# A residual tile generator queued two gate blocks later, and a smaller credit for the retention generators

## The chip, the cores and the metric

The kernel runs on one core of a Trainium2 chip. The metric is the time of one execution on the device in microseconds (us). Several executions of each kernel are timed and the median is taken; one further execution is recorded by the hardware profiler.

TensorE (PE) multiplies matrices; its weight loads (PEld) overlap its matmuls. VectorE (DVE), ScalarE (ACT) and GpSimd (POOL) do the elementwise work, and SyncE (SP) issues most of the DMA transfers. Each engine takes its instructions strictly in the order of the program that was written for it.

## What is computed

All data is float32, the sequence is 1024 tokens of width 1024 plus 256 context tokens. The computation is two chained blocks. The first has two layers; each layer projects its input, runs three mixers side by side (a short convolution, a retention in both directions, a neighbourhood attention), gates them, multiplies by an output matrix `w_out`, adds the residual and normalises:

```python
def layer_norm(x, g, b):
    xf = x.astype(F32)
    mu = jnp.mean(xf, axis=-1, keepdims=True)
    var = jnp.mean(jnp.square(xf - mu), axis=-1, keepdims=True)
    return ((xf - mu) * lax.rsqrt(var + LN_EPS) * g + b).astype(x.dtype)

def bidir_retention(q, k, v, lg_f, lg_b, s_f, s_b):
    fwd = chunk_retention(q, k, v, lg_f, s_f, True)
    bwd = chunk_retention(jnp.flip(q, 2), jnp.flip(k, 2), jnp.flip(v, 2), lg_b, s_b, False)
    return fwd + jnp.flip(bwd, 2)
```

The `... * g + b` of the first layer's normalisation over the 1024 tokens, `x1`, is the residual of the second layer; it is 8 tiles of 128 tokens by 1024. The second block mixes with a gated delta rule and a dilated attention, multiplies by `w_out2` and ends with a feed-forward network.

## The kernel before

**Products.** Each float32 product is made of three matmuls on operands split into a high and a low part (`xl·wh`, `xh·wl`, `xh·wh`, or `wh·yhl` and `wl·yhl` where the activations are the moving side). A weight tile of 128x512 goes through four steps: SP loads it (`wr`), ACT writes its high part (`wh`), POOL writes its low part (`wl = wr - wh`), PE uses both. Three buffers hold `wr`, three `wh` and three `wl`, so the splits run at most two or three tiles ahead of PE.

**The main line and the generators.** The PE program is the main line of products (projections, gate blocks, `w_out`) with pieces of other work sown between them. That other work is written as Python generators: each retention pair, each neighbourhood-attention unit, each dilated unit, and small ones such as `x1_gen`. The class `Mixer` (line 27) steps them. After each main matmul `pe` (line 212) adds the matmul's time times `ratio` to `credit`, up to 3000, and generators are stepped while the credit lasts; each step takes the PE time that the generator used from it. `add` with `now=True` starts a generator at once; without it the generator waits in queue "a" behind those added before, and `fill` starts it when fewer than `conc` run and `room()` allows it. `room()` is the number of free buffers in a pool of 40 tiles of 128x1024, less what the running generators may still take. `run_until` steps generators without a look at the credit until a condition holds: `need_room(n)` until there is room, `need_o` until a mixer's output is written, `drain` until none is left. In such a stretch PE has no main product, only generator pieces, and waits whenever these wait for DVE or ACT. We call it a drain.

**Order on the other engines.** The order of the PE program is the order in which code is emitted. On DVE, ACT, POOL and SP the order follows a number that the mixer gives each instruction from its own model clock (plus `late`, 5000 for `x1_gen`), so a change of the interleaving re-orders these queues as well.

**The layer loop.** `layer` (line 1101) walks the list `r0 r1 r2 c0 n0 c1 n1 g0 g1 n2 g2 g3 g4 g5`: r are the retention projections, c the convolution's, n those of the neighbourhood attention, g the gate blocks. `n2` begins with `need_room(9)`, a drain; `g5` begins with `need_o` and `need_room(9)`, another. Then comes `mix.drain()`, and `w_out` starts: 12 matmuls for each weight tile k, four banks `pb` with three each. `mix.ratio` is set to `R_RET` at line 1122, after the v projection, and stays through the whole list, in both layers; the code after each layer sets it back to 10.

**The generator that is moved.** `x1_gen` (line 1664) loads gamma and beta (`lnbc`), and for each of 8 tiles loads 128 rows of the normalised first layer, `xn`, does one multiply and one add on POOL, and stores the tile to `x1[0]`. In the trace its tile is called `x`. The tiles are read again by `ln_chain` (line 1520) after `w_out` of the second layer, as `lx`.

Of the kernel before, what the change touches and what calls it, by code (L numbers as in the profile page):

```python
# [26 lines left out]
class Mixer:  # L27
# [92 lines left out]
    late = 0.0  # L120
# [362 lines left out]
class Layers(Base):  # L483
# [597 lines left out]
                self.w_add(w[l, b])  # L1081
        self.down_weights(io["w_out"][l], self.token_groups(2 if l == 0 else 0))

    R_RET = 10.0
    R_NA = 10.0

    def token_groups(self, nctx):
# [13 lines left out]
    def layer(self, l, hT, need_ctx, ready=None, ready_k=None):  # L1101
        nc, io, mix = self.nc, self.io, self.mix
        self.phase(f"layer{l}")
        V = [self.S(f"rv{p}", (128, 8, 128)) for p in range(3)]
        Vc = [self.C(f"rvc{p}", (128, 2, 128)) for p in range(3)]

        def ev_v(t, c, ps):
            if c == 0:
                for p in range(3):
                    d = V[p][:, t] if t < 8 else Vc[p][:, t - 8]  # L1110
                    self.act(d, ps[:, 128 * p:128 * p + 128])
            else:
                tt = self.S("nvt", (128, 384))
                nc.vector.tensor_copy(tt, ps)
                nc.sync.dma_start(out=self.nvd[l][128 * t:128 * t + 128], in_=tt)
                self.free(tt)

        self.down(self.token_groups(2), 8, self.hT_lhs(hT), ev_v, None, 384, ready, ready_k)
        gx, gk = hT.groups(need_ctx), hT.groups(True)
        self.phase(f"ret{l}")  # L1120
        self.ret_consts(l)
        mix.ratio = self.R_RET
        self.ropeC, self.ropeS = self.S("ropeC"), self.S("ropeS")
        nc.sync.dma_start(out=self.ropeC, in_=io["c_rope"][0])
        nc.sync.dma_start(out=self.ropeS, in_=io["c_rope"][1])
        for s in self.ORDER1[l].split():
            p = int(s[1])
            if s[0] == "r":
                mix.conc = self.CR[l]
                self.ret_blocks(l, p, gx, gk, V, Vc, need_ctx)  # L1130
            elif s[0] == "n":
                mix.conc = self.CN[l]
                self.need_room(self.ROOM1[l])
                self.phase(f"na{l}.{p}")
                self.na_blocks(l, p, gx, gk, need_ctx)
            elif s[0] == "c":
                self.conv_blocks(l, p, gx, need_ctx)
            else:
                if p == 0 and l == 1:
                    mix.add(self.x1_gen(), True, peak=3, late=self.X_MOD)  # L1140
                if p == 5:
                    self.need_o(l, p)
                    self.need_room(9)
                    self.ln_setup(l, 2 if need_ctx else 1)
                    self.y_prefetch(self.token_groups(2 if need_ctx else 0)[0], self.yT[l], ROWS1, 5)
                self.gate_block(l, p, gx, need_ctx)
        self.free(*hT.tiles())
        self.phase(f"draina{l}")
        mix.drain()
        self.phase(f"drain{l}")  # L1150
# [1559 lines left out]
```

## Time and profile before

| what | value |
|---|---|
| median of 3 runs | 2963.77 us (2957.46 to 2966.71) |
| the profiled execution | 2959.18 us, of which the span in the profile is 2957.4 us |
| granted TensorE clock, mean over the span | 0.957 |
| busy: PE, DVE, ACT, POOL | 2722.3, 1985.9, 1190.1, 971.4 us |

The span is the time from the first to the last instruction that the profiler recorded; the profiled execution's own time has 1.78 us more around it. An engine's busy time leaves out its waits, so the span less PE's 2722.3 us is the time in which PE waited. A granted clock of 1.0 is TensorE's full clock (2.4 GHz), 0.5 its lower level (1.2 GHz), at which a matmul takes twice as long.

### The profile page before, as it was taken

The page shows a single profiled execution, that of the slowest core. Times are in us where ns is not written, and L with a number is a line of the kernel's source. Part 1 is how long each engine was busy: PE and PEld are TensorE (multiplying, and loading weights), DVE is VectorE, ACT ScalarE, POOL GpSimd, SP SyncE. Part 2 cuts the span into 40 slices and gives each one's busy share as a digit, 9 for nine tenths or more (in the row PEclk, how much of TensorE's full clock was granted, in tenths as well). Part 3 has the DMA queues.
Part 4 walks back from the last instruction along what each step waited for, and adds up shares of the span by engine and source line. Part 5 has one row for each costly group of instructions (what it writes and reads, how often), then busy time and mean ns, then how long its engine had stood idle before and what let it go on. Part 6 is the DMA issues. An engine that isn't in the chain of part 4 may idle for free. (4 is left out here: it accounts for less than half of the span.)

```text
span 2957.4 us, 41337 instructions
## 1 busy us (share of the span) xinstructions
PE 2722.3 (92%) x14572; PEld 2342.2 (79%) x14572; DVE 1985.9 (67%) x4011; ACT 1190.1 (40%) x2715; POOL 971.4 (33%) x836
## 2 busy tenths in 40 slices
PE   6989999999989989979999977899998999999998
PEld 6977888898788878768787766787876788887886
DVE  6866675774642557667554697868844588786687
ACT  5212254563332225445443332456653333333443
POOL 4443512213433441451563332111135244443001
PEclk9988999999999999989999979999999999999999
DMA  7533302216333221433543543222343222223874
GB/s 254 180 103 124 93 32 78 82 65 202 127 108 100 65 70 34 154 119 131 169 135 108 170 139 123 99 72 85 109 158 125 96 107 107 107 96 122 305 252 168
DMA packets 173071, 367.87 MB, mean 124 GB/s; under 512 B 30048, under 2 KB 57984, under 8 KB 172864
## 3 DMA queue, kind: packets, MB, share of 16 engines
q1 hardware_dynamic: 160064, 343.07, 34.3%
q10 hardware_dynamic: 10016, 13.12, 1.8%
q0 software_dynamic: 2784, 9.05, 1.0%
q8 instruction: 115, 1.88, 0.3%
q14 instruction: 92, 0.75, 0.1%
HBM read 279.35 MB, written 79.51 MB: 121 GB/s over the span
## 5 line engine op out<-in xcount | busy, mean ns | idle before, releaser
L251 POOL TENSOR_TENSOR wl<-wr,wh 128x512 fp32r<-128x512 f32 (+2 forms) x344 | 452.1, 1318 | 1151.0 <-ACT wh L251 1046.9
L344 PE MATMUL pb<-xl,wh 128*128 128x512 f32 x1456 | 580.2, 399 | 0.0
L344 PE MATMUL pb<-xh,wl 128*128 128x512 f32 x1456 | 579.5, 398 | 0.6 <-POOL wl L251 0.6
L344 PE MATMUL pb<-xh,wh 128*128 128x512 f32 x1456 | 579.1, 398 | 0.0
L251 ACT ACTIVATE wh<-wr 128x512 fp32r<-128x512 f32 (+2 forms) x344 | 202.7, 591 | 401.7 <-PE pb L344 314.4
L344 PEld LDWEIGHTS pb<-xh,wl 128*128 128x128 f32 x1456 | 277.6, 191 | 56.5 <-POOL wl L251 1.0
L344 PEld LDWEIGHTS pb<-xl,wh 128*128 128x128 f32 x1456 | 277.8, 191 | 54.1 <-issue 0.2
L344 PEld LDWEIGHTS pb<-xh,wh 128*128 128x128 f32 x1456 | 277.7, 191 | 53.0 <-issue 0.3
L344 PE MATMUL pb<-wh,yhl 128*128 128x512 f32 x832 | 264.0, 396 | 7.0 <-DVE xl L251 4.4
L344 PE MATMUL pb<-T,wh 128*128 128x512 f32 x640 | 196.9, 389 | 0.0
L344 PEld LDWEIGHTS pb<-wh,yhl 128*128 128x128 f32 x832 | 158.4, 191 | 41.3 <-issue 6.0
L251 POOL TENSOR_TENSOR wl<-ws,wh 128x512 fp32r<-128x512 f32 x100 | 135.0, 1350 | 155.4 <-ACT wh L251 154.0
L344 PE MATMUL pb<-wl,yhl 128*128 128x512 f32 x416 | 164.8, 396 | 5.1 <-POOL wl L251 5.1
L344 PE MATMUL pb<-whi,yhl 128*128 128x512 f32 x528 | 164.0, 392 | 4.5 <-DVE yhl L251 4.5
L251 ACT ACTIVATE pt<-pb 128x512 fp32r<-128x512 f32 (+3 forms) x230 | 114.0, 528 | 132.4 <-PE pb L349 115.5
L251 DVE TENSOR_TENSOR pt<-pb,pt 128x512 fp32r<-128x512 f32 (+3 forms) x230 | 130.0, 595 | 51.5 <-ACT pt L251 50.3
L344 PEld LDWEIGHTS pb<-T,wh 128*128 128x128 f32 x640 | 120.1, 188 | 25.0
L251 DVE TENSOR_TENSOR yhl<-yr,yhl 128x512 fp32r<-128x512 f32 (+2 forms) x133 | 97.6, 760 | 61.4 <-ACT yhl L251 52.4
L251 ACT ACTIVATE wh<-ws 128x512 fp32r<-128x512 f32 x100 | 63.2, 632 | 172.7 <-PE pb L344 172.7
L344 PE MATMUL pb<-wl,xh 128*128 128x384 f32 (+1 forms) x384 | 125.9, 328 | 5.9 <-POOL wl L251 5.9
L344 PE MATMUL pb<-wh,xl 128*128 128x384 f32 (+1 forms) x384 | 126.0, 328 | 3.4 <-ACT wh L251 1.3
L344 PE MATMUL pb<-wh,xh 128*128 128x384 f32 (+1 forms) x384 | 125.4, 327 | 0.0
(434 smaller groups left out, 6009.5 us busy)
## 6 DMA issues: line engine op xcount, KB each, us to landing
wr<-in_w_in_dram SPq DMA_DIRECT2D x152, 256.0 KB, 2.7
ws<-in_w_down_dram SPq DMA_DIRECT2D x110, 256.0 KB, 5.6
wr<-in_w_out_dram SPq DMA_DIRECT2D x96, 256.0 KB, 2.9
yr<-ffn SPq DMA_DIRECT2D x33, 512.0 KB, 5.8
wm<-in_w_modT_dram SPq DMA_DIRECT2D x32, 512.0 KB, 4.8
wr<-in_w_v_dram SPq DMA_DIRECT2D x64, 192.0 KB, 2.4
ws<-in_w_gate_dram SPq DMA_DIRECT2D x22, 512.0 KB, 5.3
ws<-in_w_up_dram SPq DMA_DIRECT2D x22, 512.0 KB, 6.1
```

Source lines behind the costliest of these rows:

```text
L251: return fn(*a, **kw)
L344: self.mix.product(c / 2.4, out, (lhsT, rhs), lambda: self.nc.tensor.matmul(out, lhsT, rhs, start=start, stop=stop))
```

## The change

Two edits, both to tables or calls of the schedule; what is computed stays the same.

```diff
@@ -1081,7 +1081,7 @@
         self.down_weights(io["w_out"][l], self.token_groups(2 if l == 0 else 0))
 
-    R_RET = 10.0
+    R_RET = 2.0
     R_NA = 10.0
 
@@ -1136,8 +1136,8 @@
             elif s[0] == "c":
                 self.conv_blocks(l, p, gx, need_ctx)
             else:
-                if p == 0 and l == 1:
-                    mix.add(self.x1_gen(), True, peak=3, late=self.X_MOD)
+                if p == 2 and l == 1:
+                    mix.add(self.x1_gen(), peak=3, late=self.X_MOD)
                 if p == 5:
                     self.need_o(l, p)
                     self.need_room(9)
```

With the first, a main matmul earns the generators a fifth of the credit in both layers' lists. With the second, the second layer's `x1_gen` is not started ahead of `g0`, but put into the queue ahead of `g2`, behind the neighbourhood-attention units that wait there. Both programs have the same instructions on PE; they stand in another order on every engine from the first layer's retention on.

**The start of the second layer's `w_out`, on POOL.** `wl_2868`, `wl_2874`, `wl_2878` and `wl_2883` are the low parts of its weight tiles k = 1 to 4. Before, they follow each other:

```order
L251 TENSOR_TENSOR wl_2792_13735<-wr_2701_13367,wh_2791_13734 128x512
L251 TENSOR_TENSOR wl_2868_13893<-wr_2787_13726,wh_2867_13892 128x512
L251 TENSOR_TENSOR wl_2874_13917<-wr_2790_13732,wh_2873_13916 128x512
L251 TENSOR_TENSOR wl_2878_13939<-wr_2866_13890,wh_2877_13938 128x512
L251 TENSOR_TENSOR wl_2883_13961<-wr_2872_13914,wh_2882_13960 128x512
```

In the changed kernel the generator's first two tiles (`x1_2743`, `x1_2759`, two instructions each) stand just ahead of `wl_2868`, and behind `wl_2874` comes:

```order
L251 TENSOR_TENSOR wl_2868_13893<-wr_2781_13696,wh_2867_13892 128x512
L251 TENSOR_TENSOR wl_2874_13917<-wr_2784_13702,wh_2873_13916 128x512
L251 TENSOR_TENSOR x1_2790_13740<-x1_2790_13740,lnbc_2741_13552 128x1024
L251 TENSOR_TENSOR x1_2790_13740<-x1_2790_13740,lnbc_2742_13553 128x1024
L251 TENSOR_TENSOR x1_2792_13773<-x1_2792_13773,lnbc_2741_13552 128x1024
```

After the same pairs for `x1_2793` to `x1_2795` the piece ends, still in the changed kernel, with

```order
L251 TENSOR_TENSOR x1_2795_13788<-x1_2795_13788,lnbc_2742_13553 128x1024
L251 TENSOR_TENSOR x1_2796_13793<-x1_2796_13793,lnbc_2741_13552 128x1024
L251 TENSOR_TENSOR x1_2796_13793<-x1_2796_13793,lnbc_2742_13553 128x1024
L251 TENSOR_TENSOR wl_2878_13939<-wr_2866_13890,wh_2877_13938 128x512
L251 TENSOR_TENSOR wl_2883_13961<-wr_2872_13914,wh_2882_13960 128x512
```

So 12 `x1` instructions moved in between the low parts of k = 2 and k = 3; before, all 16 stood among `g0` to `n2`.

**The same place on SP.** `yr_2861`, `yr_2869`, `yr_2875` are activation tiles that ACT and DVE split into `yhl`; ACT's split of `yr_2869` stands, in both kernels, just ahead of `wh_2877`, the high part of k = 3. Before:

```order
L251 DMA bcr_2856_13870<-in_g_mix_pre_dram 128x1024
L251 DMA yr_2861_13876<-yT1_5_44_159 128x512
L251 DMA yT1_7_46_161<-go_2786_13724 128x512
L251 DMA yr_2869_13908<-yT1_6_45_160 128x512
L251 DMA wr_2872_13914<-in_w_out_dram 128x512
```

And now, where `x1_0` is the DRAM tensor to which the generator stores:

```order
L251 DMA bcr_2856_13870<-in_g_mix_pre_dram 128x1024
L251 DMA x1_0_49_164<-x1_2795_13788 128x1024
L251 DMA yr_2861_13876<-yT1_5_44_159 128x512
L251 DMA x1_0_49_164<-x1_2796_13793 128x1024
L251 DMA yr_2869_13908<-yT1_6_45_160 128x512
L251 DMA wr_2872_13914<-in_w_out_dram 128x512
```

The loads of `yr_2869` and of k = 4's weights moved behind the store of the last `x1` tile, which has to wait for that tile's POOL instructions.

**The dilated attention of the second block, on PE.** `xl`, `xh` with `wh`, `wl` are main products; `dsl` are scores of a dilated unit that PE transposes. Before, a main product of the next projection follows:

```order
L344 MATMUL pb_3955_19149<-xh_3055_14713,wl_3947_19097 128x512
L344 MATMUL pb_3992_19275<-xl_2941_14222,wh_3949_19102 128x512
L344 MATMUL pb_3992_19275<-xh_2937_14218,wh_3949_19102 128x512
L344 MATMUL pb_3992_19275<-xh_2937_14218,wl_3950_19103 128x512
L344 MATMUL pb_3992_19275<-xl_2941_14222,wh_3949_19102 128x512
L344 MATMUL pb_3992_19275<-xh_2937_14218,wh_3949_19102 128x512
L349 MATMUL pb_3993_19281<-ident_107,dsl_3959_19160 128x128
```

In the changed kernel the same place begins a piece of generator work with no main product in it:

```order
L344 MATMUL pb_3955_19149<-xh_3055_14713,wl_3947_19097 128x512
L349 MATMUL pb_3984_19261<-ident_107,dsl_3959_19156 128x128
L349 MATMUL pb_3984_19261<-ident_107,dsl_3960_19157 128x128
L349 MATMUL pb_3984_19261<-ident_107,dsl_3959_19156 128x128
L349 MATMUL pb_3984_19261<-ident_107,dsl_3960_19157 128x128
L349 MATMUL pb_3986_19269<-ident_107,dsl_3959_19156 128x128
L349 MATMUL pb_3986_19269<-ident_107,dsl_3960_19157 128x128
```

That piece has 96 matmuls, and two more like it follow, of 116 and 96. Before there are none of these three, but one of 88 at the end of that stage. A longer one ahead of them has 279 matmuls before and 276 now. The pieces are drains of `need_room`: before, the `x1_gen` that was started without a look at the room left the mixer's count of free buffers one higher from then on, and the count passed there; now it does not.

## Rows read from the trace of the kernel before

**Rows 1.** The page, busy time of each engine over the span.

```profile
PE 2722.3 (92%) x14572; PEld 2342.2 (79%) x14572; DVE 1985.9 (67%) x4011; ACT 1190.1 (40%) x2715; POOL 971.4 (33%) x836
```

**Rows 2.** Stretches: length; busy PE, PEld, DVE, ACT, POOL; clock; DMA share; GB/s.

```profile
200.00:330.00 130.00, 117.14 (x771) 99.13 (x769) 97.44 (x237) 26.92 (x65) 51.47 (x42) 0.87 0.36 107
207.70:238.40 30.70, 24.71 (x126) 21.60 (x127) 27.78 (x66) 7.03 (x18) 17.13 (x11) 0.50 0.28 84
960.00:1060.00 100.00, 89.82 (x568) 73.35 (x567) 61.05 (x140) 23.82 (x52) 47.50 (x35) 0.90 0.24 59
1053.60:1057.60 4.00, 3.95 (x12) 3.31 (x13) 3.89 (x7) 0.60 (x1) 0.00 (x0) 0.50 0.17 66
540.00:575.00 35.00, 29.73 (x180) 26.60 (x179) 28.13 (x85) 20.64 (x63) 10.65 (x15) 0.90 0.22 74
555.90:562.70 6.80, 5.48 (x25) 5.19 (x26) 4.60 (x9) 1.58 (x3) 5.42 (x9) 0.50 0.40 135
1251.60:1295.20 43.60, 23.86 (x129) 22.25 (x129) 35.37 (x77) 18.61 (x53) 22.21 (x14) 0.69 0.34 115
1259.00:1279.50 20.50, 10.12 (x44) 9.44 (x44) 14.75 (x22) 5.42 (x15) 8.91 (x4) 0.50 0.26 92
1375.80:1388.30 12.50, 8.53 (x52) 7.13 (x51) 9.67 (x26) 5.77 (x15) 1.30 (x1) 0.86 0.51 175
1399.90:1431.00 31.10, 31.10 (x139) 25.76 (x138) 12.74 (x16) 12.35 (x21) 14.79 (x12) 1.00 0.55 174
1904.00:1959.50 55.50, 47.52 (x363) 44.42 (x362) 44.21 (x128) 31.55 (x82) 8.76 (x10) 0.91 0.20 63
1960.00:2172.00 212.00, 196.24 (x1113) 167.38 (x1113) 162.11 (x449) 126.28 (x288) 29.86 (x24) 0.96 0.29 97
2150.10:2167.20 17.10, 12.23 (x89) 10.40 (x87) 13.98 (x36) 9.89 (x24) 1.42 (x1) 0.99 0.28 90
2166.90:2173.80 6.90, 4.57 (x13) 3.55 (x12) 4.37 (x8) 4.86 (x10) 0.00 (x0) 0.51 0.70 226
```

**Rows 3.** Who waited for whom in the second layer's n2 drain: total, times, longest.

```profile
PE pb L349 <- DVE sl L251: 19.5, 5, 5.9
```

**Rows 4.** Timeline of DVE in that drain: start us, us, instruction.

```profile
1258.34 0.34 DVE L251 TENSOR_SCALAR sl<-sl,rsm 128x256 f32<-128x256 f32 x1
1258.60 2.42 DVE L251 TENSOR_SCALAR sc<-sc,rsm 128x256 f32<-128x256 f32 x1
```

**Rows 5.** Timeline of POOL in that drain.

```profile
1258.35 4.95 POOL L251 TENSOR_TENSOR x<-x,lnbc 128x1024 f32<-128x1024 f32 x2 [4.61 <-DMA yT<-go]
```

**Rows 6.** The tile `x`: duration ns min/median/max, first and last start.

```profile
L251 POOL TENSOR_TENSOR x<-x,lnbc x16: 2338/2384/2532, 1217.4 to 1313.8; 128x1024 f32<-128x1024 f32 x16
```

**Rows 7.** Timeline of POOL, g5 to the second layer's w_out.

```profile
1377.84 1.30 POOL L251 TENSOR_TENSOR wl<-wr,wh 128x512 fp32r<-128x512 f32 x1 [3.65 <-ACT wh L251]
...
1400.64 1.49 POOL L251 TENSOR_TENSOR wl<-wr,wh 128x512 fp32r<-128x512 f32 x1 [1.42 <-ACT wh L251]
1403.59 1.44 POOL L251 TENSOR_TENSOR wl<-wr,wh 128x512 fp32r<-128x512 f32 x1 [1.46 <-ACT wh L251]
```

**Rows 8.** Timeline of PE, first matmul of w_out and first of k = 3 with `wl`.

```profile
1399.90 0.39 PE L344 MATMUL pb<-wh,yhl 128*128 128x512 f32 x1
...
1408.29 0.39 PE L344 MATMUL pb<-wl,yhl 128*128 128x512 f32 x1
```

**Rows 9.** The tile `yr` there on SP: from issue to landing.

```profile
DMA to landing us min/median/max: 2.8/3.0/3.3
```

**Rows 10.** Timeline of ACT, one split of `yr` and one of `wr`.

```profile
1405.44 0.63 ACT L251 ACTIVATE yhl<-yr 128x512 fp32r<-128x512 f32 x1 [1.93 <-DMA yr<-yT]
1405.98 0.61 ACT L251 ACTIVATE wh<-wr 128x512 fp32r<-128x512 f32 x1
```

**Rows 11.** Timeline of PE, the longest wait of the second layer's retention.

```profile
1053.65 1.09 PE L349 MATMUL pb<-ident,O 128*128 128x128 f32 x4 [8.40 <-DVE O L251]
```

**Rows 12.** Timeline of DVE in the g5 drain.

```profile
1377.93 1.35 DVE L251 TENSOR_SCALAR sc<-sc,rsm 128x256 f32<-128x256 f32 x1
```

## The prediction

> **What bounds the kernel now.** I read the page first: PE is busy 2722.3 us, 92% of the span, its weight loads run beside that, and the next engine, DVE, has 67% [rows 1]. So PE's main line sets the time, and a change of order can only act through PE's waits (235 us in all, the span less the busy time) and through the granted clock. Next I looked for the stretches where PE waits, by the table of stretches [rows 2]. Compare length and PE's busy time in each: the two retentions (200 to 330 and 960 to 1060) leave 12.9 and 10.2 us, the drain at the second layer's `n2` (1251.6 to 1295.2) 19.7 us, the drain at `g5` 4.0 us, the stage of the dilated units (1960 to 2172) 15.8 us. The start of the second layer's `w_out` (1399.9 to 1431) leaves nothing: PE is busy 31.1 of 31.1 us. That is where the changed order puts something new.
>
> The waits of the `n2` drain end on DVE's scores `sl`: 19.5 us in five waits [rows 3]. The timeline of DVE shows why some last so long. At 1258.60 a TENSOR_SCALAR over 128x256 takes 2.42 us; the one just before, of the same size, takes 0.34 [rows 4]. POOL had begun a pair of `x1_gen`'s operations at 1258.35 [rows 5]. One such operation takes 2384 ns in the median, and there are 16 [rows 6]. So in this drain a POOL operation of `x1_gen` holds up DVE by some 2.1 us, and PE behind it.
>
> **The rule behind that row.** The Trainium skill, page "SBUF — State Buffer", section "Who interferes with whom", says that DVE and GpSimd share one pair of SBUF ports as an exclusive lock, that a DVE operation in a two-port mode or with two SBUF inputs meets a GpSimd operation that reads SBUF there, and that whoever issues first holds it for its whole instruction. The trace agrees (2.42 us beside 0.34). By this rule the operations that the change brings to `g5`'s drain would block DVE as well, twice 2.38 us for the two that lie in it, where the sum below has 4.
>
> **The change, part by part.**
>
> *1. Twelve POOL operations ahead of a weight's low part.* In the new order of POOL, 12 operations of `x1_gen` stand between the `wl` of k = 2 and that of k = 3. Before, the `wl` of k = 2 ended at 1400.64 + 1.49 = 1402.13 [rows 7]; it cannot come earlier, since its `wh` waited for a buffer that the end of `g5` frees at 1399.9. The twelve take 12 x 2.384 = 28.6 us [rows 6], so the last ends at 1430.7. Now follow SP: the load of the activation tile `yr_2869` stands behind the store of that last tile, lands 3.0 us after its issue [rows 9], is split on ACT (0.63), and only then come `wh` of k = 3 (0.61) [rows 10] and its `wl` (1.44) [rows 7]. That makes 1430.7 + 3.0 + 0.6 + 0.6 + 1.4 = 1436.3. PE's first matmul with this `wl` ran at 1408.29, 8.39 us after `w_out` began [rows 8]. The `wl` itself was written from 1403.59 to 1405.03, so it had 3.3 us to spare, and no more. PE will wait 28.0 us, with nothing to fill it: it takes its instructions in order, and the three products of k = 3 come next. The weight of k = 4 is loaded behind the same store, and is ready some 1.5 us after that of k = 3; PE needs it 2.7 us after (12 matmuls at 0.227 us between starts, from the 37 in those 8.39 us), so nothing more is added. After the 8.40 us wait [rows 11] PE ran 3.95 us of work at the clock 0.50 [rows 2], which at full clock would have taken half: 2 us more. Term: **+30**. Lower end 24 (only the 12 operations and the `wl`, 1430.7 + 1.4 - 1408.3); upper end 34, should the chain of loads and stores among the tiles (three in flight) add two landings. Below 24 it cannot go by any row: the operations take what they take, and POOL runs in order.
>
> *2. Four POOL operations around the `g5` drain.* The first two tiles' operations stand behind the `wl` written at 1377.84 to 1379.14 [rows 7], so the first pair runs at about 1379 to 1384, inside the drain (1375.8 to 1388.3); the second pair has to wait for its load and falls at the end of it or after. That such an overlap costs here too is shown by the `wl` at 1377.84: beside it a DVE operation took 1.35 us [rows 12] instead of 0.34. Two operations by 2.1 us: **+4**. Ends: 0 (DVE is idle 2.8 of 12.5 us, and may lie so that it is not met), and 8 (all four count).
>
> *3. The `n2` drain without `x1_gen`.* No `x1` operation stands there any more. The first layer's drain at the same place has none either, and there (540 to 575) PE waits 5.3 us instead of 19.7 [rows 2]: 14.4 us less. The half clock also shrinks: 10.12 us of PE work at 0.50 in 1259 to 1279.5, against 5.48 in 555.9 to 562.7; half the difference is 2.3. Term: **-17**. Ends: -10 (only the 2.1 us for each of five waits) and -25 (all 19.7 us and half of 10.12).
>
> *4. Credit 2 in place of 10.* The retentions leave 12.9 + 10.2 = 23.0 us of waits. The two big places, 6.0 us in 207.7 to 238.4 [rows 2] and the 8.40 us at 1053.65 [rows 11], are steps that come in the same order of PE before and after: there the generators are forced by a full pool of tiles or by a needed output, not by credit. That leaves 8.6 us in waits that a wider spacing may shorten. I take a third: **-3**. Ends: -9 (all of it), and +3 if generators that are fed less are still unfinished when an output is asked for. The work that hides what is postponed is the neighbourhood attention's projections and the gates, where PE is hardly ever short of products.
>
> *5. Three new drains among the dilated units.* 96 + 116 + 96 = 308 matmuls of generators stand without main products, where before they were sown in; the piece of 88 at the end goes. That piece (2150.1 to 2167.2) left PE waiting 4.87 us, 0.055 per matmul; the long one of 279 (1904 to 1959.5) 7.98, 0.029 per matmul [rows 2]. So 308 matmuls cost 17.0 or 8.8. What goes with the old piece is its 4.87, the 2.33 us of waiting in 2166.9 to 2173.8 and half of the 4.57 us run there at half clock: 9.5. The three pieces are of the same units as the one of 88, so I take its price, and its loss of clock (2.3) once: 17.0 + 2.3 - 9.5 = **+10**. Ends: -1 by the price of the long piece; +25 if each of the three pays twice that loss as well. An end on the other side, if the new order leaves none of the stage's waits, is a rival below.
>
> Sum: 30 + 4 - 17 - 3 + 10 = **+24**, on the profiled execution's own 2959.18: 2983. The median of the three runs is 4.6 above that execution, so the forecast for the median is 2963.8 + 24 = 2988.
>
> **Rivals.**
>
> *The second block pays it back.* If the new order of the dilated units leaves no wait in 1960 to 2172, 15.8 us and the 2.3 of clock go: -18 instead of +10. The sum is then 30 + 4 - 17 - 3 - 18 = -4, median 2960: no change that can be told (0.3%, 9 us, is about what a measurement of this kernel can tell from none). For it: generator work is always somewhere, and there are now three shorter places in place of one at the end. Against it: the only pieces without main products in the trace both left waits. Chance 0.11.
>
> *The other side: the retentions flow.* With a fifth of the credit each generator step has several main products ahead of it, so that DVE's chain is done when PE asks. If every wait of both retentions went (23.0 us), with half of the 24.71 and 3.95 us of work at half clock (14.3), the fourth term would be -37, the sum -10, the median 2954: faster. It decides from 36 us on, nearly all there is. Against it: the order at the two big waits is unchanged. Chance 0.08 for all ways below -9.
>
> *Credit does nothing.* If generators are always forced, the fourth term is 0 and the median 2991; it does not leave the side of the forecast. Chance 0.06.
>
> *Everything new costs its upper end.* 34 + 8 - 10 + 3 + 25 = +60: 3024. Each end is possible, all at once is not likely: 0.05.
>
> **How the numbers follow.** The forecast (the 12 operations bare on PE's path, the drain's gain smaller than that) has 0.70. Together with the last two rivals (0.06 and 0.05) that is slower 0.81; same 0.11; faster 0.08. The range leaves out about 1 in 10 on each side: from 2965, where the second block has just paid back 23 us of the sum, to 3011, where it and the drains cost 23 more.
>
> **What would show it.** Right: a gap of 24 to 34 us in PE's line at the third or fourth weight of the second layer's `w_out`, ended by POOL's `wl` or ACT's `wh`, with 12 `x` operations in a row on POOL; no DVE operation of 2.4 us in the `n2` drain, and waits of about 5 us there; two or more stretched DVE operations at `g5`; three stretches among the dilated units where PE is busy only some 70 to 85%. Wrong: a `w_out` without that gap (the twelve ran earlier, in a POOL that waited for less than I think), a gap of 40 us or more (loads and stores in series), an `n2` drain that still waits 15 us (then its waits were DVE's own chain), or second-block stretches that are shorter than before.

## The result and the profile after

The changed kernel takes 2986.86 us (median of 4 runs, 2985.82 to 2996.0) against 2963.88 us for the one before on the same chip: 23.0 us more, ratio 1.0087 with a 95% interval of 1.0062 to 1.0113. The forecast was 2988, slower. The profiled execution of the changed kernel took 2987.77 us, 28.6 more than that of before.

The page of the changed kernel, its busy times:

```profile
PE 2730.3 (91%) x14572; PEld 2344.8 (79%) x14572; DVE 1982.2 (66%) x4011; ACT 1189.0 (40%) x2715; POOL 964.1 (32%) x836
```

Against [rows 1] PE is busy 8.0 us longer with the same matmuls, so part of the loss is clock: the mean granted clock is 0.952 in place of 0.957. The rest is waiting.

Next the table of stretches of the changed kernel, columns as in [rows 2]: the second layer's retention, its `n2` drain, its `g5` drain, the stage of the dilated units from end to end, and the three new pieces in it.

```profile
971.80:1056.70 84.90, 76.12 (x533) 61.18 (x528) 56.47 (x144) 19.62 (x46) 36.44 (x28) 0.96 0.20 53
1236.30:1265.90 29.60, 22.86 (x128) 19.86 (x127) 25.02 (x72) 18.51 (x54) 10.30 (x15) 0.77 0.26 78
1347.00:1360.00 13.00, 8.48 (x60) 7.23 (x60) 9.97 (x27) 7.33 (x19) 6.00 (x3) 1.00 0.56 180
2007.15:2201.99 194.84, 170.21 (x931) 146.24 (x930) 145.57 (x420) 110.58 (x242) 22.07 (x18) 0.93 0.26 85
2017.90:2036.70 18.80, 13.87 (x97) 12.09 (x96) 17.13 (x59) 12.41 (x28) 1.29 (x1) 0.96 0.18 53
2071.40:2100.40 29.00, 20.31 (x117) 17.88 (x117) 27.19 (x82) 17.02 (x37) 1.61 (x2) 0.88 0.09 27
2150.60:2171.10 20.50, 14.73 (x96) 12.91 (x95) 17.40 (x56) 12.89 (x30) 1.27 (x1) 0.92 0.31 92
```

The `n2` drain is 29.6 us long instead of 43.6, and PE waits 6.7 us in it instead of 19.7. The `g5` drain waits 4.5 instead of 4.0. The three pieces wait 4.9, 8.7 and 5.8 us, and all ran below full clock.

At the start of `w_out`, where PE waited for nothing before, the timeline of PE in the changed kernel has two waits (in brackets: the wait and what ended it):

```profile
1378.75 0.77 PE L344 MATMUL pb<-wh,yhl 128*128 128x512 f32 x1 [8.34 <-DVE yhl L251]
1412.02 0.80 PE L344 MATMUL pb<-wh,yhl 128*128 128x512 f32 x1 [22.67 <-ACT wh L251]
```

The first stands ahead of k = 0, the second ahead of k = 3. The timelines of POOL, SP, ACT and DVE say where they come from. POOL:

```profile
1352.52 4.80 POOL L251 TENSOR_TENSOR x<-x,lnbc 128x1024 f32<-128x1024 f32 x2 [0.23 <-DVE go L251]
...
1375.71 16.23 POOL L251 TENSOR_TENSOR x<-x,lnbc 128x1024 f32<-128x1024 f32 x6 [3.47 <-DMA x<-xn]
1392.32 14.28 POOL L251 TENSOR_TENSOR x<-x,lnbc 128x1024 f32<-128x1024 f32 x6 [0.38 <-DMA x<-xn]
1412.05 1.27 POOL L251 TENSOR_TENSOR wl<-wr,wh 128x512 fp32r<-128x512 f32 x1 [5.45 <-ACT wh L251]
```

SP (a `x<-x` is a store of the generator, `yr<-yT` the load of an activation tile):

```profile
1401.90 0.32 SPq L251 DMA_DIRECT2D x<-x  x1
1402.39 0.32 SPq L251 DMA_DIRECT2D yr<-yT  x1
1406.62 0.32 SPq L251 DMA_DIRECT2D x<-x  x1
1407.03 0.38 SPq L251 DMA_DIRECT2D yr<-yT  x1
1407.51 0.74 SPq L251 DMA_DIRECT2D wr<-in_w_out_dram  x1
```

ACT:

```profile
1410.82 0.63 ACT L251 ACTIVATE yhl<-yr 128x512 fp32r<-128x512 f32 x1 [4.57 <-DMA yr<-yT]
1411.36 0.61 ACT L251 ACTIVATE wh<-wr 128x512 fp32r<-128x512 f32 x1
```

The chain is the one that was forecast: the twelve operations end at 1406.60, the store of the last tile is issued at 1406.62, the load of `yr` behind it at 1407.03, its split runs at 1410.82, the high part of k = 3 at 1411.36, and PE goes on at 1412.02. DVE shows the wait that was not forecast:

```profile
1350.18 0.35 DVE L251 TENSOR_SCALAR sc<-sc,rsm 128x256 f32<-128x256 f32 x1
...
1352.36 2.21 DVE L251 TENSOR_TENSOR pt<-pb,pt 128x512 fp32r<-128x512 f32 x4
...
1373.20 0.69 DVE L251 SCALAR_TENSOR_TENSOR go<-th,go 128x512 f32<-128x512 f32 x1 [13.97 <-DMA go<-oscr]
...
1375.86 13.88 DVE L251 TENSOR_TENSOR yhl<-yr,yhl 128x512 fp32r<-128x512 f32 x5
```

Five operations of DVE with both inputs in SBUF take 13.88 us beside the first six of POOL, 2.78 each, where such a one took 0.69 elsewhere in this stage; and POOL's six take 2.70 each, not 2.38. The operands of k = 0 come from the first of the five. Of PE's wait of 8.3 us ahead of k = 0 this lengthening makes 2.1. Most of the wait passes before the split begins: four operations of the gates (`go`) stand ahead of it in DVE's queue. PE's last gate product ended at 1370.41; the first of the four waits for its load until 1373.20, and the four end at 1375.94. In the kernel before only one such operation stands ahead of the first split, it runs 3.5 us before `w_out` begins, and PE waits for nothing there:

```profile
1396.35 0.69 DVE L251 SCALAR_TENSOR_TENSOR go<-th,go 128x512 f32<-128x512 f32 x1 [7.46 <-ACT yhl L251]
1396.96 0.69 DVE L251 TENSOR_TENSOR yhl<-yr,yhl 128x512 fp32r<-128x512 f32 x1
```

The waits at `w_out` add up to 31.6 us (8.3, 22.7, and 0.6 for the `wl` behind the second). Behind each of the two long ones PE runs at about half clock for some 5 us (granted clock 0.52 from 1378.75 to 1383.60 and from 1412.02 to 1417.80).

**The stages side by side.** The same matmul can be found in each kernel's trace, so a stage can be timed from the start of one to the start of another. The table has the stages with a lasting difference, for every kernel that was run (experiments below), from the profiled execution of each, in us. "w_out" runs from a matmul of the last gate group to one of the tenth weight tile; "second block" from the middle of the delta rule's stage to the end of the dilated units.

| kernel | retention 1 | retention 2 | n2 to g5 | w_out | second block |
|---|---|---|---|---|---|
| before | 189.3 | 90.5 | 177.7 | 27.9 | 301.7 |
| changed | 186.3 | 85.0 | 156.8 | 64.7 | 320.1 |
| changed, again (e8) | 185.7 | 85.0 | 157.0 | 64.4 | 321.9 |
| credit only (e1) | 185.8 | 86.0 | 177.2 | 28.4 | 303.8 |
| move only (e2) | 187.6 | 89.3 | 167.3 | 60.9 | 317.7 |
| changed, a tile more (e3) | 185.8 | 84.9 | 156.7 | 64.4 | 300.9 |
| before, a tile less (e4) | 187.6 | 91.3 | 178.0 | 27.9 | 321.4 |
| changed, no POOL operations (e5) | 185.9 | 84.8 | 155.9 | 51.0 | 321.2 |
| before, no POOL operations (e6) | 187.5 | 89.2 | 160.2 | 27.9 | 303.7 |
| changed, no generator (e9) | 186.0 | 84.9 | 156.0 | 29.0 | 318.5 |

From before to changed these five give -2.9, -5.6, -20.9, +36.8 and +18.4, together +25.8 of the 28.6. The other stages differ by up to some us between executions that have the same order there (in the profiled executions of all the kernels, the same early matmul stands between 106.7 and 113.1 us), so nothing is read from them. Each stage is read from one execution, which need not be the median one: the profiled execution of e3 took 6 us less than the median of its kernel, that of e1 took 6 and that of e10 11 us more.

### The profile page after: what moved, and what is told of

Read it like the earlier page. It is cut to its first block, busy times and chain, and to the rows that moved or that the text cites. A ratio compares the mean times of both kernels' runs of the same rounds, so it can differ in the third digit from the quotient of the medians.

```text
span 2986.0 us, 41306 instructions
## 1 busy us (share of the span) xinstructions
PE 2730.3 (91%) x14572; PEld 2344.8 (79%) x14572; DVE 1982.2 (66%) x4011; ACT 1189.0 (40%) x2715; POOL 964.1 (32%) x836
## 5 line engine op out<-in xcount | busy, mean ns | idle before, releaser
L344 PE MATMUL pb<-wl,yhl 128*128 128x512 f32 x416 | 167.3, 402 | 5.9 <-POOL wl L251 5.9
L251 DVE TENSOR_TENSOR yhl<-yr,yhl 128x512 fp32r<-128x512 f32 (+2 forms) x133 | 107.6, 838 | 81.3 <-ACT yhl L251 81.2
```

The source lines that it names most:

```text
L251: return fn(*a, **kw)
L344: self.mix.product(c / 2.4, out, (lhsT, rhs), lambda: self.nc.tensor.matmul(out, lhsT, rhs, start=start, stop=stop))
```

## The experiments

Expectations stand as they were written ahead of each run. Ratios are to the kernel before in the same session.

**e1, the credit alone.** Before, with

```diff
-    R_RET = 10.0
+    R_RET = 2.0
```

> Only the credit of 2, the generator started where it was before. By the forecast's fourth term 3 us less than before, ratio 0.999. By my reading of the trace of the changed kernel (2.7 us less in the first layer's retention, 5.6 in the second's) 8 us less, 0.997, with the drains of the dilated units and the gap in w_out absent. Rival, that the credit and not the move brings the drains of the second block: 10 to 20 us more, 1.003 to 1.007.

Measured: 2950.86 against 2955.86 us, ratio 0.9983 (0.9972 to 0.9994): 5 us less. Retention 1 and 2 are 3.5 and 4.5 us shorter, n2 and w_out stay, and the second block has none of the 18 us of the changed kernel. So the credit gains a little by itself and brings none of the drains.

**e2, the move alone.** Before, with

```diff
-                if p == 0 and l == 1:
-                    mix.add(self.x1_gen(), True, peak=3, late=self.X_MOD)
+                if p == 2 and l == 1:
+                    mix.add(self.x1_gen(), peak=3, late=self.X_MOD)
```

> Only the generator's move, credit 10. By the forecast's terms 30 + 4 - 17 + 10 = 27 us more than before, ratio 1.009. By the trace of the changed kernel 34 in w_out, 18 less in the n2 drain, 20 in the second block: 36 us more, 1.012. Rival, that the credit matters for where the twelve operations fall: no gap of 20 us in w_out, ratio 1.00.

Measured: 3001.49 against 2955.86 us, ratio 1.0154 (1.0135 to 1.0173): 45.6 us more, beyond either theory. The move is worse without the lower credit than with it, by more than the 5 us of e1. The stage from n2 to g5 shows where: 167.3 us, 10.5 more than in the changed kernel. The timeline of POOL in this run, and that of DVE:

```profile
1360.00 4.80 POOL L251 TENSOR_TENSOR x<-x,lnbc 128x1024 f32<-128x1024 f32 x2
```

```profile
1360.11 2.42 DVE L251 TENSOR_SCALAR sl<-sl,rsm 128x256 f32<-128x256 f32 x1
1362.45 2.50 DVE L251 TENSOR_SCALAR sc<-sc,rsm 128x256 f32<-128x256 f32 x1
...
1371.58 5.83 DVE L251 TENSOR_SCALAR dg<-ident,mod 128x128 f32<-128x128 f32 x8
```

Here the generator's first pair falls onto the TENSOR_SCALARs of the `g5` drain, and two of them take 2.4 and 2.5 us. Its second pair, which begins at 1372.39, falls onto eight small ones (`dg`), which take 5.83 us together; in the kernel before they took 1.66. In the changed kernel the last `sc`, at 1350.18, was done 2 us before the first pair began at 1352.52, the eight `dg` took 2.46 beside its end, and the second pair ran from 1362.65, when DVE had nothing to do. The same four operations of POOL cost 10 us in the one order and under 1 in the other.

**e3 and e4, the count of free tiles.** e3 is the changed kernel, e4 the one before, with one line more where the second block begins:

```diff
         self.phase("vb2")
+        heapq.heappush(mix.slots, mix.vt)    # e3
+        heapq.heappop(mix.slots)             # e4
```

> The changed kernel, with one more free tile in the mixer's count from the second block on (the count that the kernel before had there); its PE order has the two pieces of 279 and 88 matmuls again in place of 276, 96, 116 and 96. By the forecast's fifth term 10 us less than the changed kernel, ratio to before 1.005. By the trace of the changed kernel, where this stage is 20 us longer, 20 us less, ratio to before 1.001. Rival, that the second block's loss is not due to those drains: as the changed kernel, 1.009.

> The kernel before, with one free tile less in the mixer's count from the second block on; its PE order then has the pieces of 276, 96, 116 and 96 matmuls of the changed kernel, and nothing else of the change. By the forecast's fifth term 10 us more than before, 1.003. By the trace of the changed kernel 20 us more, 1.007. Rival: no difference, 1.000.

Measured: e3 2970.63 against 2955.86 us, ratio 1.0050 (1.0034 to 1.0066); e4 2978.26, ratio 1.0074 (1.0057 to 1.0091). e4, which has nothing of the change but those three pieces, is 22 us slower. The table of stretches of e4, its stage of the dilated units from end to end:

```profile
1996.10:2192.80 196.70, 173.49 (x937) 149.30 (x936) 147.97 (x422) 111.04 (x243) 22.16 (x18) 0.91 0.26 86
```

It takes 196.7 us with PE waiting 23.2, as in the changed kernel (194.8 and 24.6); the whole second block is 19.7 us longer than before. In e3 the same line takes 19 us from the changed kernel's second block in the profiled execution, the second fastest of e3's nine. By the ratios of e3 and e8 (the changed kernel again, below) its whole time is 11 us less, with some 6 to each side. That the drains come from the count alone is shown. Their size is 18 to 20 us in the stages and 22 in e4's time; e3's time gives less, and why is not known.

How the count came to differ was not tested. The section on the change puts it down to a start "without a look at the room"; but by the code `add` with `now=True` also steps the other generators until `room()` is at least `peak` less 2, here 1. What can raise the count is `new_slot`: it takes nothing off when the list of free tiles is empty, and the tile's release puts one on all the same.

**e5 and e6, the POOL operations.** The changed kernel and the one before, each without the multiply by gamma and the add of beta:

```diff
-            self.tt(x, x, gb[0], ALU.mult, self.nc.gpsimd)
-            self.tt(x, x, gb[1], ALU.add, self.nc.gpsimd)
```

> The changed kernel without the generator's 16 operations on POOL (the multiply by gamma and the add of beta of the first layer's residual are left out; its loads and stores stay). If those operations are what PE waits for at w_out (8.3 us ahead of k = 0, 22.7 ahead of k = 3 in the trace of the changed kernel), some 28 to 34 us less than the changed kernel, ratio to before 0.997 to 1.000. Rival, that the chain of loads and stores on SP holds the weights back by itself: most of the 31 us stay, 1.005 or more.

> The kernel before without the same 16 operations (same part left out). By the forecast's third term, whose cause was POOL's operations beside DVE's, 14 to 18 us less than before, ratio 0.994 to 0.995, and no DVE operation of 2 us or more in the n2 drain. Rival, that the drain's waits are DVE's own chain: 0.999 to 1.000.

Measured: e5 2971.69 against 2959.36 us, ratio 1.0037 (1.0024 to 1.0050), where the changed kernel run beside it (e8) has 1.0088; e6 2941.22 us, ratio 0.9930 (0.9916 to 0.9945). e6 gains 20.7 us, a little more than expected: the operations are what made the `n2` drain dear. e5 gains 15 us only; neither theory was right. In the timeline of PE in e5 both waits are still there, 5.2 and 11.1 us long in place of 8.3 and 22.7:

```profile
1373.74 0.77 PE L344 MATMUL pb<-wh,yhl 128*128 128x512 f32 x1 [5.17 <-DVE yhl L251]
1395.68 0.79 PE L344 MATMUL pb<-wh,yhl 128*128 128x512 f32 x1 [11.11 <-ACT wh L251]
```

And SP in e5:

```profile
1373.43 1.90 SPq L251 DMA_DIRECT2D x<-x  x3
1375.38 2.99 SPq L251 DMA_DIRECT2D x<-xn  x3
1381.65 3.21 SPq L251 DMA_DIRECT2D x<-x  x3
1384.95 0.39 SPq L251 DMA_DIRECT2D bcr<-in_g_mix_pre_dram  x1
1385.56 0.92 SPq L251 DMA_DIRECT2D yr<-yT  x1
```

A store waits on SP until its tile has been loaded, a load until a buffer is free, and the activation tiles and weights of `w_out` stand behind all of them. That holds k = 3. Ahead of k = 0 DVE has the same four gate operations before its split as in the changed kernel, and the split itself is not lengthened here.

**e8, the changed kernel again**, as the base for these runs.

> The changed kernel once more, as the base for the runs beside it: 1.0087 to before, as measured, within 0.003.

Measured: 2986.54 against 2959.36 us, ratio 1.0088 (1.0074 to 1.0102).

**e9, no generator.** The changed kernel with the generator's start taken out; the second layer's residual is then the first layer's normalised tile without gamma and beta:

```diff
-                if p == 2 and l == 1:
-                    mix.add(self.x1_gen(), peak=3, late=self.X_MOD)
...
-            return self.ln_chain(1, t, self.x1[0][128 * t:128 * t + 128], fin)
+            return self.ln_chain(1, t, self.xn[128 * t:128 * t + 128], fin)
```

> The changed kernel without the generator at all: the second layer reads the first layer's normalised tiles before gamma and beta as its residual (the multiply, the add, and the loads and stores of the generator are left out). With the operations gone alone, 16 of the 31 us of waiting at w_out stayed. If the loads and stores on SP hold those, w_out has no wait here and the kernel is some 28 to 31 us under the changed one, ratio to before 0.998 to 1.000. Rival, that the order of the splits at w_out holds PE also without the generator: 1.003 as with the operations gone.

Measured: 2951.96 against 2959.95 us, ratio 0.9974 (0.9965 to 0.9982), 0.0114 or 34 us under e8's, a little more than expected. `w_out` takes 29.0 us; what is left of the two waits, in the timeline of PE, is

```profile
1371.53 0.47 PE L344 MATMUL pb<-wh,yhl 128*128 128x512 f32 x1 [0.88 <-DVE yhl L251]
```

So of the 36 us between e9 and the changed kernel at `w_out`, 22 stay when only the operations go (e5) and leave when the transfers go too. With the generator gone the order on DVE changes back as well: as in the kernel before, one gate operation stands ahead of the first split. How much of the 22 is the transfers' and how much that order's, e9 does not tell; in e5 the wait behind the transfers is 11.1 us, the one for DVE's split 5.2.

**e7, e10 and e11, the generator earlier.** Credit 2; the generator starts ahead of `n0` of the second layer (e7) or ahead of its v projection (e10, e11), in place of the start at `g0`. e10 has the line of e3 as well:

```diff
+            if l == 1 and s == "n0":                                           # e7
+                mix.add(self.x1_gen(), True, peak=3, late=self.X_MOD)
...
+        if l == 1:                                                             # e10, e11
+            mix.add(self.x1_gen(), True, peak=3, late=self.X_MOD)
         self.down(self.token_groups(2), 8, self.hT_lhs(hT), ev_v, None, 384, ready, ready_k)
```

> Credit 2, and the generator started ahead of n0 of the second layer, where main products are plenty: its 16 POOL operations then stand before the n2 drain, none between the weights of w_out, and the dilated units have pieces of 229 and 88 matmuls without main products. If the terms are as the traces say (nothing in w_out, 15 to 18 less in n2, 5 to 8 less for the credit, nothing in the second block) 20 to 26 us less than before, ratio 0.991 to 0.993. Rival, that DVE is as much in the way at n0 as at n2: 0.998 or more.

> Credit 2, the generator started ahead of the second layer's v projection, where PE waits for nothing in 130 us and POOL is busy 51 of them, and one more free tile in the count from the second block on. Its operations stand one or two at a time between low parts of weights. By the measured terms: 18 to 20 less for the n2 drain and g0, 5 less for the credit, 0 at w_out, 0 in the second block: 23 to 25 us less than before, ratio 0.992. Rival, that single operations of 2.4 us delay the low parts there as twelve in a row did at w_out: 0.997 or more.

> As the run beside it, without the added tile in the count, so with the pieces of 276, 96, 116 and 96 matmuls in the second block. If these cost 18 to 22 us wherever the generator stands, that much more than the run beside it: ratio to before 0.998 to 1.000. Rival, that their price hangs on the rest of the change: less than 12 us more.

Measured: e7 2952.42 against 2959.36 us, ratio 0.9977 (0.9967 to 0.9987); e10 2946.07 against 2959.95, ratio 0.9963 (0.9949 to 0.9977); e11 2966.15, ratio 1.0020 (1.0010 to 1.0030). All three lose the waits at `n2` and none has one of note at `w_out`, yet e7 and e10 gain 7 and 11 us where over 20 were expected, and e11 is slower than the 0.998 to 1.000 expected of it. In e7 the stretch from the end of the second retention to `n2` came out 25 us longer: PE has pieces of generator work there and waits of up to 4.5 us for DVE's `sl`, and two operations of DVE take 2.28 and 2.38 us beside POOL's; before, PE waits for nothing in that stretch. POOL in e10, during the v projection, and the wait of PE there:

```profile
881.35 7.12 POOL L251 TENSOR_TENSOR x<-x,lnbc 128x1024 f32<-128x1024 f32 x3 [3.46 <-DMA x<-xn]
888.43 0.99 POOL L251 TENSOR_TENSOR wl<-wr,wh 128x384 fp32r<-128x384 f32 x1
```

```profile
889.48 0.69 PE L344 MATMUL pb<-wl,xh 128*128 128x384 f32 x1 [5.29 <-POOL wl L251]
```

Three operations in a row ahead of one low part are enough for a wait of 5.3 us; the v projection and the first products of `r0` behind it came out 14 us longer (in an execution 11 us above e10's median). e11 is 0.0057 or 17 us over e10, the price of the drains once more. e10 and e7 are faster than both kernels, and so is e1.

## Why the prediction was right, point by point

The time and its direction came out, and at the `w_out` of k = 3, in the `n2` drain and among the dilated units the cause was the one named. That the median came within 2 us of the forecast is luck: by the stages of the profiled executions two terms were 7 and 8 us too small, and `g5`, `n2` and the credit were 4 to 6 too high each.

*1. w_out, +30 forecast, 36.8 in the stage.* The place, the ender (`wh` of k = 3 behind the load of `yr_2869` behind the last store) and the twelve operations in a row are in the trace. The wait ahead of k = 3 is 22.7 us, below the 24 under which it could not go "by any row": the forecast counted the twelve from 2.2 us after the start of `w_out`, and they ran from 1375.71, 3.0 us ahead of it, because `w_out` itself began late. That is what the forecast left out. It let k = 0 to k = 2 run freely; in fact PE waited 8.3 us ahead of k = 0, 2.8 of it until the load for DVE's gate operations had landed, 2.7 while the four of them ran that the new order has ahead of the split (before, one), and 2.1 because the split, with both inputs in SBUF, shares its time with POOL's operations. The second start at half clock was not counted either. The Trainium skill's rule of the shared port pair (page "SBUF — State Buffer", "Who interferes with whom") names this kind of DVE operation; the forecast applied the rule to `g5` and not here, where the trace agrees with it (2.78 us each beside POOL, 0.69 without). And the forecast priced the wait by POOL's operations. e5 shows that without them, with the generator's loads and stores on SP and the new order on DVE, `w_out` still takes 23 us more than before (51.0 against 27.9); with the operations it is 37.

*2. g5, +4 forecast, nearly nothing.* The first pair ran in the drain as forecast, but after the last of its 128x256 TENSOR_SCALARs; the sign of two or more stretched ones there did not come. e2 shows the term as it was described, two operations that take 2.4 and 2.5 us, and with the second pair's part 10.5 us in the stage from n2 to g5, more than the term's upper end of 8. It was a matter of 2 us in time.

*3. The n2 drain, -17 forecast.* The stage from n2 to g5 is 20.9 us shorter; PE's waits in the drain fell by 13.0. e6 shows that POOL's operations were the cause: without them the same stage loses 17.5 us, with the start at `g0` and the credit unchanged. Where the other 3.4 come from was not told apart.

*4. The credit, -3 forecast, about -5 (e1).* The interval, 2 to 8 us, holds the forecast. In the stages retention 1 takes 186 us with a credit of 2 and 188 to 189 with 10, retention 2 takes 85 to 86 and 89 to 91. The longest wait there stayed, as the forecast had said (8.04 us for DVE's `O`).

*5. The dilated units, +10 forecast, 18 to 22 (18 to 20 by the stages of the changed kernel, e3 and e4, 22 by e4's time, 17 by e11 against e10; e3's time gives 11).* The stage of the dilated units before, from the same matmul to the same as in the changed kernel's line above:

```profile
1996.10:2174.33 178.23, 163.15 (x934) 140.35 (x933) 148.68 (x422) 111.94 (x245) 22.88 (x18) 0.95 0.30 101
```

It grew by 16.6 us, of which 9.5 are waits of PE (24.6 in place of 15.1) and 7.1 are busy time for the same work, at a clock of 0.93 in place of 0.95. The waits came out: 17.0 for the new pieces, less the 4.87 and the 2.33 that were to end, are 9.8. The term that was mis-sized is the clock: it was put at 2.3 for the three pieces together and 2.3 were taken off for the old one, so at nothing. In e4 the busy time grows by 10.3. The upper end of the term counted that clock for each piece (by its words 23.6; it says 25).

That the waits agree is in part chance. The three pieces wait 19.4 us, near the 17.0 worked out from the old piece's price, but 4.8 of it, at 2076.20, is a wait for `dQ` that also stood in the kernel before, outside any such piece. Who waited for whom there before, in 1960 to 2172:

```profile
PE pb L344 <- ACT dQ L251: 5.9, 1, 5.9
```

And the wait for `yhl` behind the old piece, which was to end with it, stayed, in the changed kernel

```profile
2197.88 0.47 PE L344 MATMUL pb<-wh,yhl 128*128 128x512 f32 x1 [3.90 <-DVE yhl L251]
```

None of the rivals took place. The second block did not pay back, and the retentions gave 8.5 us in the profiled executions, not 36. The last rival, all upper ends at once, failed with the credit and `g5`.

What stays open: how the move's price splits with and without the credit. e2 and e8 differ by 0.0066 or 20 us, their profiled executions by 13.7. There e2 loses 10 in the stage from n2 to g5, 4 in the second retention and 2 in the first, and is 4 shorter each at `w_out` and in the second block; the rest lies in stages that differ by that much between executions anyway.

## What to carry to other kernels

A generator that is out of the way on PE is not out of the way: its elementwise operations sit in one engine's queue and its transfers in another's, and both queues also feed the main line. Before moving such work, read on each queue what stands behind it, and count the transfers apart from the operations: here `w_out` took 23 us more with the operations gone and the transfers left (e5). The move also re-orders queues that the generator does not use: a part of the wait ahead of k = 0 came from DVE's own gate operations in a new order. And a scheduler that counts free buffers can answer a change in one stage with drains in another; the way to price them is to change the count alone.

## What the runs showed of the hardware

POOL and DVE slow each other in pairs of operations that read SBUF: DVE's 128x512 TENSOR_TENSOR with two SBUF inputs went from 0.69 to 2.78 us and POOL's 128x1024 one from 2.38 to 2.70 while both ran, so they seem to have taken turns operation by operation. DVE's TENSOR_TENSOR with one input in PSUM kept its time beside the same POOL operations: the four `pt` that ran in the changed kernel beside the pair of 1352.52 took 2.21 us, as the four of before did with POOL idle.
